# Two-layer decoder trunk on one core: convolution weights taken pair by pair, rotary angles two stages on, the build's load times reckoned from the release of the buffers

## The chip, the cores and the metric

The kernel runs on one core of a Trainium2 chip. The metric is the device time of one execution in microseconds (us), the median of the runs shown. Three runs of the kernel before took 801.74, 802.57 and 802.96 us.

## The reference, cut to what matters

256 tokens of width 1024 go through two layers, beside a memory of 256 tokens. Everything is float32. The stage around the change is the convolution mixer of layer 0: a projection of the normed tokens to three times 1024 columns (b, c and u), a gate, a causal convolution of three taps down the tokens, a second gate, and a projection back. The rotary angles are used only in layer 1.

```
def short_conv_mixer(h, w_in, w_conv, w_out):
    b_gate, c_gate, u = jnp.split(h @ w_in, 3, axis=-1)
    z = c_gate * u
    conv = lax.conv_general_dilated(
        z, w_conv[:, None, :].astype(z.dtype), window_strides=(1,),
        padding=[(CONV_W - 1, 0)], dimension_numbers=("NWC", "WIO", "NWC"),
        feature_group_count=D_MODEL)
    return (b_gate * conv) @ w_out

...
    for l in range(DEPTH):
        h = rms_norm(x, norm_mix[l])
        if l < N_A:
            x = x + short_conv_mixer(h, conv_w_in[l], conv_w[l], conv_w_out[l])
        else:
            j = l - N_A
            x = x + moba_attention(h, moba_w_q[j], moba_w_o[j], cos, sin, k_blk, v_blk, k_mean)
        x = x + mem_cross_attention(rms_norm(x, norm_mem[l]), rms_norm(mem, norm_memkv[l]),
                                    mem_w_q[l], mem_w_kv[l], mem_w_o[l])
        x = x + swiglu(rms_norm(x, norm_ffn[l]), ffn_w_gu[l], ffn_w_down[l])
        if l == N_A - 1:
            k_blk, v_blk, k_mean = shared_kv(x, kv_norm, w_kv, cos, sin)
    return rms_norm(x, norm_final)
```

## The kernel before, in words

Every weight is used once, in chunks of 128 x 1024 float32 values (512 KB), in one order for the whole program: the list `plan` (built above line 415). A chunk passes through four stations.

- **Load.** `load_chunk` (line 347) issues the DMA on SP's queue into one of five buffers (`RAWS`), named `raw_wc`, `raw_wu` and so on. A buffer comes free when the low half of the chunk five places earlier has been made.
- **High half.** ACT casts the chunk to the type fp32r that TensorE multiplies in: `hi_wc` (`split_high`, line 367).
- **Low half.** DVE subtracts the high half from the chunk: `lo_wc` (`split_low`). High and low halves lie in ten pairs of buffers (`WBUFS`).
- **Product.** TensorE makes each product out of three: activation high by weight high, activation low by weight high, activation high by weight low. The activations are split in the same way, ACT casting and DVE subtracting; `mix` holds the normed tokens of the convolution, high and low.

All matmuls are recorded at one line, 315 (`mm`), all transposes at 319, nearly all work of ACT and DVE at 103 (a wrapper), all loads at 332. So groups are told apart by the names of their tiles.

**What sets the order.** Each engine works through its row strictly in order, and the row is fixed when the program is built. The build keeps a clock of its own, by a cost per instruction (`Clock`, line 45): `free["pe"]` is "now", `writes` says when a tile will be ready. After each matmul it calls `Side.poll` (line 138), which steps the side jobs (generators for normalising, gating, copying out of PSUM) whose time has come; a job that yields a number asks to be stepped that many ns later, and `hold` (line 156) makes one wait until a buffer is free by the build's clock. `poll` then calls `Feed.pump` (line 206), which puts the next low half into DVE's row or the next high half into ACT's row if the build's clock has its input ready by then and the engine free. `Feed.take` (line 221) is what the matmuls call: it returns a chunk's two halves and, if they are not in the rows yet, puts them there at once, with all chunks ahead of them.

**The convolution** (`short_conv`, line 875) runs over four pairs of column groups `jp`. A pair has six chunks: two each of `wc`, `wu` and `wb` (512 rows x 256 columns). The loop inside runs over the two columns `jj` of the pair, 128 wide: the matmuls of c into one of two PSUM banks `cu`, those of u into the other, those of b into a bank `pb`. When the c and u sums stand, the jobs `gate_sum` and `conv` copy both banks out (ACT copies the first token half, DVE adds the second product part: `conv <- cu`), which frees them for the next column; then come the gate, the taps and the second gate. The stage starts while the keys of the memory (`memk`) are still being made: the four `pt_h` are transposes of the normed tokens, one set for each quarter of `mix`. `pt_c` transposes two small tables, the gains (`g_rows`) and the taps (`cw_rows`); their job is `tables` (line 783).

**The angles** (`angles`, line 804) load the 256 positions, multiply them by 16 constants that GpSimd writes, reduce the result to the range of the sine with short DVE instructions on `ang` and `turns`, and take sines by ACT, which needs a table load first. The job is started at line 1337, ahead of the convolution, and asks for 15000 ns before it reads the positions. `start_rstd` (line 608) squares the memory for its norm and asks for 9000 ns first.

Behind the convolution come its output projection (`cout`), the values of the memory (`memv`), the memory attention (`mq`, `mo`) and the feed-forward layer (`swiglu`): eleven steps `jp` of two columns each, with gate and up chunks `wg` and `wu`, sums in the same two PSUM banks (now named `gu`), copies `gu_sb`, and the down projection `wd`. Layer 1 has the same stages with the block attention in place of the convolution.

Of the kernel before, what the change touches and what calls it, by code (L numbers as in the profile page):

```python
# [107 lines left out]
class Side:  # L108
# [47 lines left out]
    def hold(self, kind):  # L156

        free = self.free[kind]
        while not free or min(free) > self.clock.now:
            yield 0 if not free else min(free) - self.clock.now  # L160
        free.remove(min(free))
# [11 lines left out]
class Feed:  # L173
# [3 lines left out]
    def __init__(self, clock, items, load, high, low):  # L177
        self.clock, self.items, self.load, self.high, self.low = clock, items, load, high, low
        self.loaded = self.highs = self.lows = self.taken = self.freed = 0
        self.raw, self.ready = {}, {}  # L180
        self.hooks = {}
        self.limit = 5
# [16 lines left out]
    def next_low(self):  # L199
        n = self.lows  # L200
        self.low(self.items[n], self.raw.pop(n), *self.ready[n])
        self.lows += 1
        self.load_to(self.lows + RAWS)
# [51 lines left out]
def yoco_kernel(  # L255
# [23 lines left out]
    clock = Clock()  # L279
# [5 lines left out]
    def acc_tile(name):  # L285
        return ps_acc.tile([P, 512], F32, tag="acc", name=name)
# [44 lines left out]
    def load(dst, src, queue=None):  # L331
        (queue or nc.sync).dma_start(dst, src)
        clock.free["dma"] = max(clock.free["dma"], clock.now + 1100)
        clock.note("dma", 1.43 * math.prod(dst.shape[1:]), [dst], [], 900)
# [12 lines left out]
    def load_chunk(it):  # L347
# [3 lines left out]
        for i in range(it["pieces"]):  # L351
            load(raw[:, :, i * n:(i + 1) * n], src[:, :, i * n:(i + 1) * n])
# [255 lines left out]
    def start_rstd():  # L608
        yield 9000
# [194 lines left out]
    def angles():  # L804
# [6 lines left out]
        yield 15000  # L811
# [62 lines left out]
    def short_conv(act, into):  # L874
# [35 lines left out]
        for jp in range(4):  # L910
            wc, wu, wb = ([feed.take(f"{name}_{jp}_{g}") for g in range(2)] for name in ("wc", "wu", "wb"))
            for jj in range(2):
# [3 lines left out]
                for w in (wc, wu):  # L916
                    side.grab("gu")
                    cus.append(gu_tile("cu"))
                    mm_cols(cus[-1], act, w, jj, 0)
                pb = acc_tile("pb").rearrange("p (r t) -> p r t", r=2)  # L920
                mm_cols(pb, act, wb, jj, 0, (0,))
                for i, w in enumerate((wc, wu)):
                    mm_cols(cus[i], act, w, jj, 1)
# [413 lines left out]
    side.start(angles())  # L1337
    side.finish(x_job[0])
    short_conv(in_mix.act, in_mem0)
    memv0 = mem_values("memv0", mT0)  # L1340
# [28 lines left out]
```

## Time and profile before

| what | value |
|---|---|
| median of three runs | 802.57 us (801.74 to 802.96) |
| the profiled execution | 804.97 us, of which the span is 803.2 us |
| busy share of the span: TensorE (PE) | 98% (789.1 us) |
| weight loads into TensorE (PEld, beside PE) | 86% |
| DVE / ACT / GpSimd (POOL) | 66% / 54% / 2% |
| TensorE's granted clock, mean over the span | 0.993 of full speed |
| read from HBM | 142.64 MB, 182 GB/s with what is written |

The span is the time from the first to the last recorded instruction of the profiled execution; its own time holds 1.8 us around that. A clock of 1.00 is 2.4 GHz; the other level is 1.2 GHz, and a mean between them says for what part of a stretch each was granted. Idle time of an engine in the timeline stands in brackets behind the instruction that ended it, with what that instruction waited for last.

### The profile page before, as it was taken

Reading aid. Unit: us, or ns where it says so; the run is one execution under the profiler, and the core shown is the slowest. Engines: PE = TensorE matmul, PEld = TensorE weight load, DVE = VectorE, ACT = ScalarE, POOL = GpSimd, SP = SyncE. Lnnn points to the kernel's source line nnn. Section 1 sums busy time; section 2 is a strip of 40 time slices with the busy share of each in tenths; the row PEclk is TensorE's granted clock in tenths of the full one; section 3 lists DMA queues with packets and bytes.
Section 4 is the critical chain, followed back from the end, with each engine's and each line's share of the span. In section 5 each row is a group of like instructions: output and inputs, shape, how many; then the busy total and the mean of one; then the engine's idle time right before and its main releaser. Section 6 shows DMA issues by size and latency. Waiting matters only on the chain.

```text
span 803.2 us, 11672 instructions
## 1 busy us (share of the span) xinstructions
PE 789.1 (98%) x4477; PEld 690.6 (86%) x4477; DVE 532.7 (66%) x830; ACT 436.8 (54%) x727; POOL 17.8 (2%) x44
## 2 busy tenths in 40 slices
PE   8899999999999999999999999999999999999996
PEld 8888788898898888888888889888989988888885
DVE  5888788666756656665765667877757555665553
ACT  6656646565645445554655664556645544554442
POOL 0100001000000000000010000010000000000000
PEclk9999999999999999999999999999999999999999
DMA  9666685833536654666474535667344465466611
GB/s 332 196 191 213 215 269 190 280 136 105 173 97 224 213 185 157 188 212 208 153 236 172 170 106 168 226 206 243 119 121 155 156 212 180 158 203 214 209 55 53
DMA packets 91085, 146.55 MB, mean 182 GB/s; under 512 B 4941, under 2 KB 70549, under 8 KB 90773
## 3 DMA queue, kind: packets, MB, share of 16 engines
q1 hardware_dynamic: 90276, 142.92, 54.8%
q0 software_dynamic: 288, 2.10, 0.7%
q8 instruction: 35, 0.57, 0.3%
q10 hardware_dynamic: 464, 0.79, 0.3%
q14 instruction: 22, 0.17, 0.1%
HBM read 142.64 MB, written 3.15 MB: 182 GB/s over the span
## 4 chain that ended last, share of the span: by engine, by line
PE 88%; DMA 5%; DVE 3%; ACT 2%; issue 1%; SPq 0%; POOLq 0%; ACTq 0%; DVEq 0%
PE gu L315 30%; PE ff L315 14%; PE q_acc L315 6%; PE acc_memv L315 5%; PE acc_mo L315 5%; PE acc_memk L315 3%; PE acc_v L315 3%; PE acc_q L315 3%; PE acc_k L315 3%; PE acc_o L315 3%; PE acc_cout L315 3%; PE cu L315 2%; DMA raw_wu<-in_conv_w_in_dram 2%; PE po L315 2%; PE s L315 2%
## 5 line engine op out<-in xcount | busy, mean ns | idle before, releaser
L315 PE MATMUL ff<-hi_wd,guT 128*128 128x512 f32 (+1 forms) x352 | 107.6, 387 | 0.0
L103 DVE TENSOR_TENSOR gu_sb<-gu_sb,gu 128x256 f32<-128x256 f32 x72 | 30.1, 421 | 97.0 <-ACT gu_sb L103 96.2
L103 ACT COPY gu_sb<-gu 128x256 f32<-128x256 f32 x72 | 26.4, 371 | 101.6 <-PE gu L315 101.5
L315 PEld LDWEIGHTS ff<-hi_wd,guT 128*128 128x128 f32 x352 | 65.9, 188 | 12.2
L103 ACT CAST hi_wu<-raw_wu 128x1024 fp32r<-128x1024 f32 x52 | 54.6, 1050 | 33.5 <-DMA raw_wu<-in_ffn_w_gu_dram 23.0
L315 PE MATMUL gu<-ffn,hi_wg 128*128 128x512 f32 x288 | 71.9, 391 | 0.4 <-DVE gu_sb L103 0.4
L315 PE MATMUL gu<-ffn,hi_wu 128*128 128x512 f32 x288 | 71.2, 389 | 0.0
L315 PE MATMUL ff<-lo_wd,guT 128*128 128x512 f32 (+1 forms) x176 | 68.5, 389 | 0.0
L103 DVE TENSOR_TENSOR lo_wu<-raw_wu,hi_wu 128x1024 fp32r<-128x1024 f32 x52 | 62.8, 1219 | 4.6 <-ACT hi_wu L103 4.5
L315 PEld LDWEIGHTS gu<-ffn,hi_wu 128*128 128x128 f32 x288 | 54.1, 188 | 11.3
L315 PEld LDWEIGHTS gu<-ffn,hi_wg 128*128 128x128 f32 x288 | 53.6, 188 | 11.6 <-DVE gu_sb L103 0.8
L103 DVE TENSOR_TENSOR lo_wd<-raw_wd,hi_wd 128x1024 fp32r<-128x1024 f32 x44 | 53.1, 1219 | 0.0
L103 DVE TENSOR_TENSOR lo_wg<-raw_wg,hi_wg 128x1024 fp32r<-128x1024 f32 x44 | 52.2, 1219 | 0.7 <-ACT hi_wg L103 0.5
L103 ACT CAST hi_wd<-raw_wd 128x1024 fp32r<-128x1024 f32 x44 | 45.6, 1050 | 2.8 <-DMA raw_wd<-in_ffn_w_down_dram 2.8
L315 PE MATMUL acc_memk<-mT,hi_memk 128*128 128x256 f32 x256 | 46.7, 287 | 0.0
L103 ACT CAST hi_wg<-raw_wg 128x1024 fp32r<-128x1024 f32 x44 | 44.6, 1051 | 0.6 <-PE acc_mo L315 0.6
L315 PEld LDWEIGHTS gu<-ffn,lo_wg 128*128 128x128 f32 x288 | 39.3, 190 | 2.8
L315 PE MATMUL acc_mo<-hi_mo,oT_mem 128*128 128x512 f32 x128 | 41.2, 397 | 0.2 <-DVE oT_mem L103 0.2
L315 PE MATMUL gu<-ffn,lo_wu 128*128 128x256 f32 x288 | 40.4, 283 | 0.0
L315 PE MATMUL gu<-ffn,lo_wg 128*128 128x256 f32 x288 | 40.2, 282 | 0.0
L315 PE MATMUL acc_memv<-hi_memv,mT 128*128 128x512 f32 x128 | 39.7, 391 | 0.0
L315 PEld LDWEIGHTS acc_memk<-mT,hi_memk 128*128 128x128 f32 x256 | 39.5, 193 | 0.2
(230 smaller groups left out, 1722.3 us busy)
## 6 DMA issues: line engine op xcount, KB each, us to landing
raw_wg<-in_ffn_w_gu_dram SPq DMA_DIRECT2D x44, 512.0 KB, 5.7
raw_wu<-in_ffn_w_gu_dram SPq DMA_DIRECT2D x44, 512.0 KB, 3.6
raw_wd<-in_ffn_w_down_dram SPq DMA_DIRECT2D x44, 512.0 KB, 4.8
raw_memv<-in_mem_w_kv_dram SPq DMA_DIRECT2D x16, 512.0 KB, 4.9
raw_mq<-in_mem_w_q_dram SPq DMA_DIRECT2D x16, 512.0 KB, 5.3
raw_mo<-in_mem_w_o_dram SPq DMA_DIRECT2D x16, 512.0 KB, 5.4
raw_memk<-in_mem_w_kv_dram SPq DMA_DIRECT2D x14, 512.0 KB, 5.4
raw_wc<-in_conv_w_in_dram SPq DMA_DIRECT2D x8, 512.0 KB, 3.8
```

What stands on the lines that cost most here:

```text
L103: return call(out, *args, **kw)
L315: nc.tensor.matmul(o, l, r, start=start, stop=stop)
```

## The change

It has five parts.

- **Weights pair by pair.** `short_conv` took all six chunks of a pair at its top. Now `conv_w` takes two chunks when the first matmul that needs them is written: wc, then wu, then wb.
- **Angles.** `side.start(angles())` moves from ahead of the convolution to behind it, so the job runs beside the first value projection; its first wait drops from 15000 to 4000 ns.
- **Loads in the build's clock.** `Feed` notes in `emptied` when the low half that frees a buffer is done, and `load` starts its reckoning of that chunk's DMA no earlier than that (`freed`). Chunks of column weights (`rows=False`) are reckoned at 1.9 ns a value where it was 1.43.
- **`hold`** no longer waits again if the build's clock has not moved since it last looked.
- **`start_rstd`** asks for 7000 ns where it asked for 9000.

```
--- before.py
+++ after.py
@@ -156,7 +156,9 @@
     def hold(self, kind):
 
         free = self.free[kind]
-        while not free or min(free) > self.clock.now:
+        seen = None
+        while not free or min(free) > self.clock.now != seen:
+            seen = self.clock.now if free else None
             yield 0 if not free else min(free) - self.clock.now
         free.remove(min(free))
 
@@ -178,6 +180,7 @@
         self.clock, self.items, self.load, self.high, self.low = clock, items, load, high, low
         self.loaded = self.highs = self.lows = self.taken = self.freed = 0
         self.raw, self.ready = {}, {}
+        self.emptied = 0.0
         self.hooks = {}
         self.limit = 5
 
@@ -200,6 +203,7 @@
         n = self.lows
         self.low(self.items[n], self.raw.pop(n), *self.ready[n])
         self.lows += 1
+        self.emptied = self.clock.last
         self.load_to(self.lows + RAWS)
 
     def pump(self, soon):
@@ -328,10 +332,10 @@
         side.poll()
         mm(o, a[0], b[0], False, stop, ns)
 
-    def load(dst, src, queue=None):
+    def load(dst, src, queue=None, rows=True, freed=0.0):
         (queue or nc.sync).dma_start(dst, src)
-        clock.free["dma"] = max(clock.free["dma"], clock.now + 1100)
-        clock.note("dma", 1.43 * math.prod(dst.shape[1:]), [dst], [], 900)
+        clock.free["dma"] = max(clock.free["dma"], clock.now + 1100, freed + 1100)
+        clock.note("dma", (1.43 if rows else 1.9) * math.prod(dst.shape[1:]), [dst], [], 900)
 
 
 
@@ -349,7 +353,7 @@
         src = it["src"].rearrange("(a p) n -> p a n", p=P)
         n = it["b"] // it["pieces"]
         for i in range(it["pieces"]):
-            load(raw[:, :, i * n:(i + 1) * n], src[:, :, i * n:(i + 1) * n])
+            load(raw[:, :, i * n:(i + 1) * n], src[:, :, i * n:(i + 1) * n], rows=it["a"] == 1, freed=feed.emptied)
         return raw
 
     def split(hi, lo, src):
@@ -606,7 +610,7 @@
         rstd_from(ss, m_rs[:, h:h + 1])
 
     def start_rstd():
-        yield 9000
+        yield 7000
         yield from mem_rstd(m0, 0)
         yield
         yield from mem_rstd(m1, 1)
@@ -808,7 +812,7 @@
         pos_i = const.tile([P, 2], I32, name="pos_i")
         with nc.allow_non_contiguous_dma(reason="256 positions"):
             nc.sync.dma_start(pos_i, positions[0].rearrange("(h p) -> p h", p=P))
-        yield 15000
+        yield 4000
         pos_f = const.tile([P, 2], F32, name="pos_f")
         vector.tensor_copy(pos_f, pos_i)
         ang = const.tile([P, 2, HR], F32, name="ang")
@@ -908,19 +912,26 @@
             yield
 
         for jp in range(4):
-            wc, wu, wb = ([feed.take(f"{name}_{jp}_{g}") for g in range(2)] for name in ("wc", "wu", "wb"))
+            taken = {}
+
+            def conv_w(name):
+                if name not in taken:
+                    taken[name] = [feed.take(f"{name}_{jp}_{g}") for g in range(2)]
+                return taken[name]
+
             for jj in range(2):
                 j = 2 * jp + jj
                 pieces = [feat.tile([P, T], F32, tag=f"f{i}", name=f"conv{i}") for i in range(2)]
                 jobs, cus = [], []
-                for w in (wc, wu):
+                for name in ("wc", "wu"):
                     side.grab("gu")
                     cus.append(gu_tile("cu"))
-                    mm_cols(cus[-1], act, w, jj, 0)
+                    mm_cols(cus[-1], act, conv_w(name), jj, 0)
                 pb = acc_tile("pb").rearrange("p (r t) -> p r t", r=2)
+                wb = conv_w("wb")
                 mm_cols(pb, act, wb, jj, 0, (0,))
-                for i, w in enumerate((wc, wu)):
-                    mm_cols(cus[i], act, w, jj, 1)
+                for i, name in enumerate(("wc", "wu")):
+                    mm_cols(cus[i], act, conv_w(name), jj, 1)
                     if jj:
                         feed.free(2)
                     jobs.append(side.start(gate_sum(cus[0], pieces[0]) if i == 0 else conv(j, cus[1], pieces, jobs)))
@@ -1334,9 +1345,9 @@
     in_mem0, in_mem1, in_moba = Plain("mem0", "mem0"), Plain("mem1", "mem1"), Plain("moba")
     in_ffn0, in_ffn1 = Normed("ffn0", norm_ffn[0]), Normed("ffn1", norm_ffn[1])
 
-    side.start(angles())
     side.finish(x_job[0])
     short_conv(in_mix.act, in_mem0)
+    side.start(angles())
     memv0 = mem_values("memv0", mT0)
     mem_attention(0, memk0, memv0, in_mem0, in_ffn0)
     swiglu(0, in_ffn0, residual(in_moba))
```

The last three parts change only numbers in the build's clock; what they do is seen in the rows of the engines. Names are those of the program, with the pair, the half of the rows (0 or 1) and a running number. Lines of the changed kernel are four higher than before.

**The start of the convolution.** ACT's row from the first high halves of the first pair's wu on, before:

```order
L103 CAST hi_wu_0_467<-raw_wu_0_406 128x1024
L103 CAST hi_wu_1_486<-raw_wu_1_443 128x1024
L103 CAST mix_0_292<-pt_h 128x4x128
L103 CAST memk_u_482<-k_sb 128x2x256
L103 CAST hi_wb_0_517<-raw_wb_0_462 128x1024
L103 CAST mix_1_293<-pt_h 128x4x128
L103 CAST hi_wb_1_562<-raw_wb_1_501 128x1024
```

and now:

```order
L103 CAST hi_wu_0_484<-raw_wu_0_402 128x1024
L103 CAST memk_u_489<-k_sb 128x2x256
L103 CAST mix_1_297<-pt_h 128x4x128
L103 CAST hi_wu_1_523<-raw_wu_1_453 128x1024
L103 CAST hi_wb_0_556<-raw_wb_0_461 128x1024
L103 CAST memk_u_489<-k_sb 128x2x256
L103 CAST hi_wb_1_588<-raw_wb_1_506 128x1024
```

The last cast of `mix` (the second row of that name) stood behind the first `hi_wb`; now both `hi_wb` and the second `hi_wu` stand behind it. On TensorE the same place, before:

```order
L315 MATMUL acc_memk_3_184<-mT_1_114,lo_memk_7_420 128x256
L315 MATMUL cu<-mix_0_292,hi_wc_0_431 128x512 x4
L315 MATMUL cu<-mix_1_293,hi_wc_1_445 128x512 x4
L315 MATMUL cu<-mix_0_292,hi_wu_0_467 128x512
L319 MATMUL pt_c<-ident,g_rows_541 128x32
L319 MATMUL pt_c<-ident,cw_rows 128x24
L315 MATMUL cu<-mix_0_292,hi_wu_0_467 128x512 x3
L315 MATMUL cu<-mix_1_293,hi_wu_1_486 128x512 x4
L315 MATMUL pb<-mix_0_292,hi_wb_0_517 128x512
```

and now:

```order
L319 MATMUL acc_memk_3_184<-mT_1_114,lo_memk_7_420 128x256
L319 MATMUL cu<-mix_0_296,hi_wc_0_437 128x512 x4
L319 MATMUL cu<-mix_1_297,hi_wc_1_467 128x512 x4
L319 MATMUL cu<-mix_0_296,hi_wu_0_484 128x512 x4
L319 MATMUL cu<-mix_1_297,hi_wu_1_523 128x512 x2
L323 MATMUL pt_c<-ident,g_rows_543 128x32
L323 MATMUL pt_c<-ident,cw_rows 128x24
L319 MATMUL cu<-mix_1_297,hi_wu_1_523 128x512 x2
L319 MATMUL pb<-mix_0_296,hi_wb_0_556 128x512
```

The transposes `pt_c` stood behind one matmul of the second weight, wu; now they stand behind six of it. Ahead of the rows shown, the fourth set of transposes `pt_h` had 12 matmuls of `memk` between itself and the first `cu`; now it has 28. On SP the loads keep their order but for that of the positions, which stood between the two loads of the second pair's wc and now stands behind the third load of `mq`.

**The second and third pair.** DVE's row around the third pair's first column (pairs count from 0 in the names, so `lo_wu_2` is the third pair's), before:

```order
L103 TENSOR_TENSOR lo_wc_2_1_815<-raw_wc_2_1_774,hi_wc_2_1_814 128x1024
L103 TENSOR_TENSOR conv0_870<-conv0_870,cu_872 128x256
L103 TENSOR_TENSOR conv1_871<-conv1_871,cu_886 128x256
L103 TENSOR_TENSOR conv0_870<-conv0_870,conv1_871 128x256
L103 TENSOR_TENSOR lo_wu_2_0_833<-raw_wu_2_0_777,hi_wu_2_0_832 128x1024
L103 TENSOR_TENSOR lo_wu_2_1_854<-raw_wu_2_1_780,hi_wu_2_1_853 128x1024
L103 TENSOR_TENSOR lo_wb_2_0_945<-raw_wb_2_0_783,hi_wb_2_0_944 128x1024
L103 TENSOR_TENSOR lo_wb_2_1_964<-raw_wb_2_1_864,hi_wb_2_1_963 128x1024
```

and now:

```order
L103 TENSOR_TENSOR lo_wc_2_1_805<-raw_wc_2_1_746,hi_wc_2_1_804 128x1024
L103 TENSOR_TENSOR yT_0_562<-conv1_752,yT_0_562 128x256
L103 TENSOR_TENSOR lo_wu_2_0_831<-raw_wu_2_0_767,hi_wu_2_0_830 128x1024
L103 TENSOR_TENSOR conv0_838<-conv0_838,cu_840 128x256
L103 TENSOR_TENSOR lo_wu_2_1_853<-raw_wu_2_1_782,hi_wu_2_1_852 128x1024
L103 TENSOR_TENSOR conv1_839<-conv1_839,cu_857 128x256
L103 TENSOR_TENSOR conv0_838<-conv0_838,conv1_839 128x256
L103 TENSOR_TENSOR lo_wb_2_0_893<-raw_wb_2_0_786,hi_wb_2_0_892 128x1024
```

Here `conv <- cu` is the second half of a copy out of a `cu` bank. `lo_wu_2_1`, whose end lets the load of the fourth pair's `raw_wu_3_0` go out, stood behind both copies and their product; now it stands between the two. On ACT `hi_wu_3_0` stands ahead of both copies of the next column, as before, and the sines and the table load, which stood in ACT's row of this pair, have gone to the value projection.

**A feed-forward step.** ACT's row in the fifth step of layer 0, before:

```order
L103 CAST hi_wu0_4_0_2793<-raw_wu0_4_0_2702 128x1024
L103 CAST hi_wu0_4_1_2803<-raw_wu0_4_1_2760 128x1024
L103 COPY gu_sb0_2764<-gu_2766 128x256
L103 COPY gu_sb1_2765<-gu_2785 128x256
L103 ACTIVATE gu_sb0_2764<-gu_sb0_2764 128x256
L103 CAST guT0_1_2609<-gu_sb1_2765 128x256
```

and now:

```order
L103 CAST hi_wu0_4_0_2793<-raw_wu0_4_0_2697 128x1024
L103 COPY gu_sb0_2764<-gu_2766 128x256
L103 CAST hi_wu0_4_1_2822<-raw_wu0_4_1_2760 128x1024
L103 COPY gu_sb1_2765<-gu_2785 128x256
L103 ACTIVATE gu_sb0_2764<-gu_sb0_2764 128x256
L103 CAST guT0_1_2609<-gu_sb1_2765 128x256
```

The high half of the second chunk of wu stood ahead of both copies out of the banks; now it stands between them. This is so in 14 of the 22 steps of the two layers.

## Rows read from the trace of the kernel before

**Rows 1.** TensorE's waits: what waits <- for whom: us in all, times, longest.
```profile
PE cu L315 <- DVE mix L103: 2.2, 1, 2.2
PE cu L315 <- DVE conv L103: 2.1, 1, 2.1
```

**Rows 2.** Stretches: from:to, length, busy PE, PEld, DVE, ACT, POOL; granted clock, DMA share, GB/s.
```profile
34.65:37.04 2.39, 0.19 (x2) 0.00 (x1) 0.75 (x2) 2.31 (x3) 0.00 (x0) 1.00 0.72 226
37.04:42.09 5.05, 5.05 (x15) 3.81 (x16) 5.05 (x6) 1.75 (x3) 0.00 (x0) 0.66 0.44 124
79.92:82.21 2.29, 0.18 (x2) 0.01 (x1) 0.48 (x2) 1.83 (x4) 0.00 (x0) 1.00 1.06 353
82.21:87.57 5.36, 5.36 (x16) 4.28 (x17) 4.94 (x10) 2.10 (x5) 0.00 (x0) 0.68 0.10 31
```

**Rows 3.** Timeline, ACT and DVE ahead of the first wait: start, us, instruction.
```profile
34.73 1.04 ACT L103 CAST hi_wb<-raw_wb 128x1024 fp32r<-128x1024 f32 x1 [2.50 <-DMA raw_wb<-in_conv_w_in_dram]
35.68 0.58 ACT L103 CAST mix<-pt_h 128x512 fp32r<-128x512 f32 x1
...
36.29 0.69 DVE L103 TENSOR_TENSOR mix<-pt_h,mix 128x512 fp32r<-128x512 f32 x1 [2.13 <-ACT mix L103]
```

**Rows 4.** Timeline, ACT and DVE ahead of the second wait.
```profile
64.44 1.06 ACT L103 CAST hi_wu<-raw_wu 128x1024 fp32r<-128x1024 f32 x1 [0.68 <-DMA raw_wu<-in_conv_w_in_dram]
...
68.50 1.28 ACT L103 ACT_TABLE_LOAD   x1
...
71.80 2.35 DVE L103 TENSOR_TENSOR lo_wu<-raw_wu,hi_wu 128x1024 fp32r<-128x1024 f32 x2
...
80.38 1.04 ACT L103 CAST hi_wu<-raw_wu 128x1024 fp32r<-128x1024 f32 x1 [2.82 <-DMA raw_wu<-in_conv_w_in_dram]
```

**Rows 5.** Timeline, SP's queue: loads issued.
```profile
31.29 1.54 SPq L332 DMA_DIRECT2D g_rows<-in_norm_mem_dram  x1
...
34.23 0.40 SPq L332 DMA_DIRECT2D raw_wc<-in_conv_w_in_dram  x1
...
74.22 1.47 SPq L332 DMA_DIRECT2D raw_wu<-in_conv_w_in_dram  x2
```

**Rows 6.** Timeline, TensorE around the first wait.
```profile
31.88 0.60 PE L319 MATMUL pt_h<-ident,hn 128*128 128x128 f32 x4
...
33.74 1.09 PE L315 MATMUL cu<-mix,hi_wc 128*128 128x512 f32 x4
...
38.41 0.31 PE L319 MATMUL pt_c<-ident,g_rows 32*128 32x32 f32 x1
```

**Rows 7.** Timeline, TensorE in the third pair's first column.
```profile
67.11 1.12 PE L315 MATMUL cu<-mix,lo_wc 128*128 128x256 f32 x8
```

**Rows 8.** DMA issues from 31.2 to 35.5 us: count, KB each, us to landing.
```profile
raw_wc<-in_conv_w_in_dram SPq DMA_DIRECT2D x1, 512.0 KB, 3.8
g_rows<-in_norm_mem_dram SPq DMA_DIRECT2D x1, 8.0 KB, 5.1
```

**Rows 9.** Timeline, DVE, TensorE and ACT: an angle's instruction, the first value projection.
```profile
59.65 0.19 DVE L103 SCALAR_TENSOR_TENSOR ang<-turns,ang 128x32 f32<-128x32 f32 x1
...
126.31 3.67 DVE L103 SCALAR_TENSOR_TENSOR lo_memv<-raw_memv,g_cols,hi_memv 128x1024 fp32r<-128x1024 f32 x3
...
132.09 0.39 PE L315 MATMUL acc_memv<-lo_memv,mT 128*128 128x512 f32 x1
...
135.60 1.28 DVE L103 SCALAR_TENSOR_TENSOR lo_memv<-raw_memv,g_cols,hi_memv 128x1024 fp32r<-128x1024 f32 x1
...
137.39 1.28 DVE L103 SCALAR_TENSOR_TENSOR lo_memv<-raw_memv,g_cols,hi_memv 128x1024 fp32r<-128x1024 f32 x1
...
143.06 1.31 ACT L103 ACTIVATE memv<-acc_memv,m_rs 128x512 fp32r<-128x512 f32 x2 [5.99 <-PE acc_memv L315]
```

**Rows 10.** Timeline, ACT and TensorE in a feed-forward step of layer 1.
```profile
754.85 1.06 ACT L103 CAST hi_wu<-raw_wu 128x1024 fp32r<-128x1024 f32 x1 [1.31 <-DMA raw_wu<-in_ffn_w_gu_dram]
...
761.08 1.98 PE L315 MATMUL gu<-ffn,hi_wu 128*128 128x512 f32 x8
```

More of the change, by code (lines that the diff above doesn't have):

```diff
@@ L158, in hold @@
         free = self.free[kind]
-        while not free or min(free) > self.clock.now:
+        seen = None
+        while not free or min(free) > self.clock.now != seen:
+            seen = self.clock.now if free else None
             yield 0 if not free else min(free) - self.clock.now
@@ L180, in __init__ @@
         self.raw, self.ready = {}, {}
+        self.emptied = 0.0
         self.hooks = {}
@@ L202, in next_low @@
         self.lows += 1
+        self.emptied = self.clock.last
         self.load_to(self.lows + RAWS)
@@ L329, in mm3, with load @@
         mm(o, a[0], b[0], False, stop, ns)
-    def load(dst, src, queue=None):
+    def load(dst, src, queue=None, rows=True, freed=0.0):
         (queue or nc.sync).dma_start(dst, src)
-        clock.free["dma"] = max(clock.free["dma"], clock.now + 1100)
-        clock.note("dma", 1.43 * math.prod(dst.shape[1:]), [dst], [], 900)
+        clock.free["dma"] = max(clock.free["dma"], clock.now + 1100, freed + 1100)
+        clock.note("dma", (1.43 if rows else 1.9) * math.prod(dst.shape[1:]), [dst], [], 900)
     def row_plan(name, w, c0, gain=None, pieces=1, halves=1):
@@ L351, in load_chunk @@
         for i in range(it["pieces"]):
-            load(raw[:, :, i * n:(i + 1) * n], src[:, :, i * n:(i + 1) * n])
+            load(raw[:, :, i * n:(i + 1) * n], src[:, :, i * n:(i + 1) * n], rows=it["a"] == 1, freed=feed.emptied)
         return raw
@@ L910, in short_conv, with conv_w @@
         for jp in range(4):
-            wc, wu, wb = ([feed.take(f"{name}_{jp}_{g}") for g in range(2)] for name in ("wc", "wu", "wb"))
+            taken = {}
+            def conv_w(name):
+                if name not in taken:
+                    taken[name] = [feed.take(f"{name}_{jp}_{g}") for g in range(2)]
+                return taken[name]
             for jj in range(2):
@@ L915, in short_conv @@
                 jobs, cus = [], []
-                for w in (wc, wu):
+                for name in ("wc", "wu"):
                     side.grab("gu")
                     cus.append(gu_tile("cu"))
-                    mm_cols(cus[-1], act, w, jj, 0)
+                    mm_cols(cus[-1], act, conv_w(name), jj, 0)
                 pb = acc_tile("pb").rearrange("p (r t) -> p r t", r=2)
+                wb = conv_w("wb")
                 mm_cols(pb, act, wb, jj, 0, (0,))
-                for i, w in enumerate((wc, wu)):
-                    mm_cols(cus[i], act, w, jj, 1)
+                for i, name in enumerate(("wc", "wu")):
+                    mm_cols(cus[i], act, conv_w(name), jj, 1)
                     if jj:
```

6 lines of the change are left out of this document (3 added, 3 removed).

## The prediction, made before the changed kernel ran

> **What bounds the kernel now.** I read the page's busy shares first, then TensorE's waits, then stretches around the two longest, then the timelines of the engines behind them. TensorE is busy 98% of the span, as the table above has it: only what it waits for, or does at a lowered clock, can be won. Two waits stand out, both in the short convolution, of 2.2 and 2.1 us [rows 1]; the reader is to see that both name DVE, which only passes on a delay. The stretches [rows 2] give their whole price. From 34.65 to 37.04 TensorE issues nothing new: 2.39 us. The next 5.05 us run at a mean granted clock of 0.66, so 5.05 x 0.34 = 1.72 us more are lost. From 79.92 to 82.21 it is 2.29 us, and 5.36 x 0.32 = 1.72 us in the stretch behind. Together 8.12 us, 1% of the run, is all that this change can reach. A difference of 0.2%, 1.6 us, is about what a measurement of this kernel can tell from none.
>
> What is late each time? The first wait is for the last quarter of the normed activations: TensorE needs its low half, which DVE makes at 36.29 out of a high half that ACT makes at 35.68, because ACT stood until 34.73 before a high half of wb whose load had not landed [rows 3]. ACT works its row strictly in order, so a weight that TensorE needs much later held back an activation it needed at once: the build had put all six chunks of the pair into the row when the first was wanted. In the second, ACT stands until 80.38 before a high half of wu [rows 4], and behind it stand the two copies that empty the PSUM banks TensorE wants. That load was issued at 74.22 [rows 5] and took 6.16 us; it could not go out earlier because its buffer was released by the low halves of wu, which DVE did only at 71.80. And they were late because ACT was busy with a table load at 68.50 for the rotary angles [rows 4] while DVE's next row waited for it.
>
> **The change, part by part.** *Weights pair by pair, first wait.* In the new order TensorE's last transposes of the normed rows stand 28 matmuls ahead of the convolution instead of 12. Before, they began at 31.88 and the convolution at 33.74 [rows 6], so 12 matmuls and 4 transposes took 1.86 us; 16 matmuls more at no more than 0.13 put them at about 29.9, done at 30.4. ACT's last cast no longer has hi_wb ahead of it: 0.58 us [rows 3], done near 31.0. DVE's low half then has one low half of wc ahead of it (2.35 for two of that size [rows 4], so 1.2) and one of memk, which is as large as mix's (0.69, and its own 0.69 behind it), so it ends by about 33.6. TensorE needs it behind four matmuls, at 34.65 (the four from 33.74 on take 0.228 each). Margin 1 us: the wait of 2.39 goes, and with it, as I take it, the lowered clock behind: 4.11 us.
>
> *Second wait.* Everything from there on runs 4.1 us earlier on TensorE, so the loads must be earlier too. The low half of wu that frees the buffer now stands right behind the first column sum of its column, ahead of the second. That sum needs the matmuls that ended at 67.11 + 1.12 = 68.2 [rows 7], now 64.1; a copy and a sum of 128x256, 0.8 us (the wait for the second ended so: ACT's high half out at 81.4, TensorE on at 82.21): 64.9. Its high half ended at 65.5 [rows 4] and can hardly be later than that now. So the low half runs from 65.5 at worst, 1.2 us, and the load goes out at 66.7 instead of 74.22. With the old 6.16 us it lands at 72.9, the high half ends at 73.9, copies and sums at 74.9. TensorE wants the bank at 79.92 - 4.11 = 75.8. Margin 0.9 us at worst. The order of ACT itself has not changed there: hi_wu still stands ahead of both copies, so this rests on the load alone. I take the 2.29 and the 1.72 as gone: 4.01 us. What is late next is this same load, by a margin of 0.9.
>
> *A new wait.* The two small transposes for the gain and tap columns (pt_c) move from behind one matmul of the second weight to behind six: TensorE reaches them at 33.74 + 14 x 0.228 = 36.9, where the old stall had let it come at 38.41 [rows 6]. Their loads go out behind a load of wb that waits for the low half of the first wc; DVE now has one more activation low half ahead of that one (0.69 us, some 0.6 in a row [rows 3]). The first of the small loads was issued at 31.29, the big one behind all of them at 34.23 [rows 5]; they landed 5.1 and 3.8 us later [rows 8], at 36.4 and 38.0, and the last small one lies between. Moved by 0.6 that is 37.0 to 38.6, against 36.9: a wait of 0.1 to 1.7 us, at the upper end with a lowered clock behind (1.7 + 1.72 = 3.4). The last small load has 12 KB (24 x 128 values) and follows the first directly, so it is nearest to the low end: I take 0.2 us.
>
> *Rotary angles two stages on.* From the convolution go twelve short DVE instructions (0.19 us [rows 9]) and the table load with four activations; they come back in the first value projection. Most stand ahead of the last low half there, which ended at 137.39 + 1.28 = 138.7. Twelve times 0.19 make that 141.0 at worst; TensorE begins this projection at 132.09 and takes six matmuls a chunk, so it wants the eighth at 132.09 + 42 x 0.228 = 141.7 [rows 9]. ACT has 5.99 us of idle time behind its squares there, ahead of 143.06, for a table load of 1.28. On SP the positions' load now stands behind the third load of query weights, which goes out once the low halves begun at 126.31 are through, at 130.0. Even if it takes 5.1 us, as the small load above, it lands at 135.1, and DVE converts the positions behind the second last low half (135.60 + 1.28 [rows 9]), at about 136.8. GpSimd's 16 constants move along between two of its powers, and nothing but the angles reads them. So I cost all this at nothing; the cover is 0.7 us on DVE and 1.7 us on the load, and past these TensorE would wait for the excess.
>
> *Loads timed from their buffers' release.* It only changes the build's own clock, and so what it puts where: in each feed-forward step ACT's high half of the second wu chunk now stands between the two copies, and DVE's low half ahead of the activation's. TensorE's row there has no idle time ahead of it (761.08 [rows 10]): cost nothing, see the last rival. No load changes its place on SP but the positions', and no instruction is added or dropped on TensorE.
>
> Sum: 2.39 + 1.72 + 2.29 + 1.72 - 0.2 = 7.9 us. The profiled execution took 804.97 us (span 803.2), so a profiled one of the changed kernel would take 797.1. The runs' median is 802.57, 2.40 below the profiled execution; taking the same off it gives 794.7.
>
> **Rivals.** *The second wait stays* (0.08): the load lands after more than 7.1 us instead of 6.16, and hi_wu still stands ahead of the copies. For it speaks that TensorE now asks for the same weights 4 us sooner; against it, that the load goes out 7.5 us sooner. Saved: 2.39 + 1.72 - 0.2 = 3.9, 798.7.
>
> *The small transposes hold TensorE* (0.08), at the upper bound: 8.12 - 3.4 = 4.7 saved, 797.9.
>
> *The clock does not hang on the waits* (0.04). The stretches show it at 1.00 up to the end of either wait and lowered right behind [rows 2], which is why I count 3.44 us for it; if it fell for another reason, only the waits go: 4.68 - 0.2 = 4.5, 798.1. The Trainium skill, "TensorE: Matmul & The Clock Gate", section "HAM oscillation — how this bites in real kernels", ties a fall to gaps of the array longer than these two; by that rule neither wait of 2.3 us would have lowered the clock, and the 3.44 us would stay. This trace does not agree with it: the lowered clock begins right behind each of these gaps.
>
> *Runs without a profile hold less of it* (0.08): if the 2.40 us between the profiled execution and the median all lie in these waits, 7.9 - 2.4 = 5.5 are saved, 797.1.
>
> *Slower* (0.03): in the feed-forward layers. The high half of wu that ACT waits for (1.31 us, until 754.85 [rows 10]) now stands between the copy of the gate bank and that of the up bank, at 14 places of the two layers. Should its load land later than now, the up copy is late with it. TensorE takes that bank again at 761.08; copy and sum ahead of it need 0.8 us and the high half 1.06, so nothing shows until the load lands at 759.2, 4.4 us later than it did. Past that point every microsecond counts 14 times: 1 us gives 802.57 - 7.9 + 14 = 808.7. Against it: DVE's low half stands earlier in its row, so the next load goes out earlier.
>
> **How the numbers follow.** The forecast has 0.69 and gives 794.7; its own range, from no new wait with the spread of the runs shown to a wait of 1.7 without a lowered clock, is 793.2 to 796.4. Adding the two rivals at 797.1 and 797.9 and the clock's at 798.1 leaves out 0.11; the range is 793.2 to 798.2. All these and the 798.7 are faster by over 0.2%: with the forecast 0.97, of which I leave 0.02 to a wait that none of them names and that eats most of the gain. So faster 0.95, within 0.2% 0.02, slower 0.03.
>
> **What would show it.** Right: among TensorE's waits the lines on mix and conv are gone; the stretches of the convolution stand at a clock of 1.00; the two copies behind the fourth pair's first high half of wu come near 74 and ACT waits less than 1 us ahead of that high half; the table load stands past 120 us, with no wait of TensorE near it; and all behind the convolution stands about 8 us earlier. Wrong: a line on pt_c of over 0.5 us, a wait on conv that stays, a clock below 1.00 somewhere between 30 and 100 us without a wait ahead of it, or a new line on gu in both feed-forward layers.

## The result and the profile after

The changed kernel took 796.93 us (median of four runs, 796.64 to 797.55), the kernel before 802.15 us (four runs, 800.34 to 802.96); the ratio is 0.9939, 95% interval 0.9920 to 0.9958. That is 5.2 us less where 7.9 were forecast; the time lies inside the forecast range and 2.2 us above the forecast itself. The two profiled executions stand further apart: 804.97 before, 796.64 now, 8.3 us.

TensorE's waits in the changed kernel (what waited <- for whom, us in all, times, longest):

```profile
PE warm L323 <- POOL neg_half L525: 1.4, 1, 1.4
PE pt_m L323 <- DMA m<-in_mem_dram: 0.5, 1, 0.5
PE acc_mo L319 <- DVE oT_mem L103: 0.2, 1, 0.2
PE pt_r L323 <- ACT qT L103: 0.2, 1, 0.2
```

Both lines of [rows 1] are gone, and none on `pt_c` or `gu` has come. Stretches of the changed kernel (columns as in [rows 2]):

```profile
34.64:38.05 3.41, 3.41 (x16) 2.56 (x15) 3.14 (x6) 1.90 (x3) 0.00 (x0) 1.00 0.72 204
75.90:79.75 3.85, 3.85 (x18) 3.19 (x17) 3.78 (x8) 0.78 (x2) 0.00 (x0) 1.00 0.53 184
```

Where [rows 2] had 0.66 and 0.68, the granted clock is 1.00. The run cut in two where the first value projection begins, before, and then the second part of the changed kernel:

```profile
0.00:132.09 132.09, 125.73 (x735) 111.21 (x736) 100.75 (x169) 80.27 (x131) 6.09 (x31) 0.97 0.72 233
132.09:803.20 671.11, 663.35 (x3743) 579.42 (x3741) 431.97 (x662) 356.48 (x596) 11.76 (x13) 1.00 0.53 173
```

```profile
124.05:794.90 670.85, 663.43 (x3743) 579.36 (x3741) 431.79 (x674) 357.07 (x601) 11.75 (x13) 1.00 0.53 172
```

In the changed kernel the projection begins at 124.05 (132.09 in [rows 9]), and 794.9 - 124.05 = 670.85 us are left. So 8.04 of the 8.3 us lie ahead of it, where the two waits and their lowered clock stood; all that stands behind it, the feed-forward layers with their changed ACT and DVE rows among it, took 0.3 us less and lost nothing.

The timeline of the changed kernel, TensorE, then ACT, DVE and SP (start, us, instruction):

```profile
33.73 2.00 PE L319 MATMUL cu<-mix,hi_wc 128*128 128x512 f32 x8
...
37.03 0.24 PE L323 MATMUL pt_c<-ident,g_rows 32*128 32x32 f32 x1
...
75.90 1.98 PE L319 MATMUL cu<-mix,hi_wc 128*128 128x512 f32 x8
...
124.05 0.39 PE L319 MATMUL acc_memv<-lo_memv,mT 128*128 128x512 f32 x1
...
30.71 0.58 ACT L103 CAST mix<-pt_h 128x512 fp32r<-128x512 f32 x1
...
71.07 1.06 ACT L103 CAST hi_wu<-raw_wu 128x1024 fp32r<-128x1024 f32 x1 [0.74 <-DMA raw_wu<-in_conv_w_in_dram]
72.62 0.37 ACT L103 COPY conv<-cu 128x256 f32<-128x256 f32 x1 [0.49 <-PE cu L319]
73.58 0.37 ACT L103 COPY conv<-cu 128x256 f32<-128x256 f32 x1 [0.59 <-PE cu L319]
...
128.74 1.28 ACT L103 ACT_TABLE_LOAD   x1
...
31.80 0.68 DVE L103 TENSOR_TENSOR mix<-pt_h,mix 128x512 fp32r<-128x512 f32 x1
...
131.14 1.28 DVE L103 SCALAR_TENSOR_TENSOR lo_memv<-raw_memv,g_cols,hi_memv 128x1024 fp32r<-128x1024 f32 x1
...
66.31 2.29 SPq L336 DMA_DIRECT2D raw_wu<-in_conv_w_in_dram  x2
```

The last cast of `mix` is done at 31.3 and its low half at 32.5; TensorE asks at 34.64. The load of the fourth pair's wu goes out at 66.31 where it went out at 74.22 [rows 5], and its high half begins at 71.07 where it began at 80.38 [rows 4]. The copies now wait for TensorE, not TensorE for them.

### The profile page after: what moved, and what is told of

Its sections match the earlier page's. It is cut to its first block, busy times and chain, and to the rows that moved or that the text cites. A ratio compares the mean times of both kernels' runs of the same rounds, so it can differ in the third digit from the quotient of the medians.

```text
span 794.9 us, 11651 instructions
## 1 busy us (share of the span) xinstructions
PE 785.6 (99%) x4477; PEld 688.7 (87%) x4477; DVE 531.0 (67%) x830; ACT 435.9 (55%) x727; POOL 18.0 (2%) x44
## 4 chain that ended last, share of the span: by engine, by line
PE 98%; DMA 0%; DVE 0%; ACT 0%; POOLq 0%; issue 0%; ACTq 0%
PE gu L319 31%; PE ff L319 15%; PE acc_memk L319 6%; PE q_acc L319 6%; PE cu L319 6%; PE acc_memv L319 5%; PE acc_mo L319 5%; PE pb L319 3%; PE acc_v L319 3%; PE acc_k L319 3%; PE acc_o L319 3%; PE acc_cout L319 3%; PE acc_q L319 3%; PE po L319 2%; PE s L319 2%; PE pt_h L323 1%
```

## The experiments

Two theories stood against each other. A is the prediction's: taking the weights pair by pair frees the cast of `mix`, and the angles' move helps the second wait. B holds that the loads' reckoning, costed at nothing in the prediction, moves the rows. Medians are given beside that of before in the same job, which differs from job to job (801.80, 802.35, 803.45 and 801.96 us).

### The same kernels once more

> The kernel before, unchanged, once more. The profiled execution of before took 804.97 us, while its four other runs took 800.34 to 802.96 and those of the changed kernel only 796.64 to 797.55. Theory (the two waits of the convolution, and the lowered clock behind them, differ from execution to execution, because both end with the landing of a load): the times spread over 2 us or more again, the granted clock of the runs lies between 0.992 and 0.997, longer where it is lower, and the new profile shows waits of TensorE on mix and conv that differ by over 0.5 us from 2.2 and 2.1. Rival (the waits are fixed, and only that one execution was disturbed elsewhere): waits of 2.2 and 2.1 again, within 0.2, and times within 1 us of each other.

Twelve runs: 802.12 us (801.39 to 805.12), ratio 1.0011 (0.9999 to 1.0023). The profiled execution took 801.39. Its waits and stretches:

```profile
PE cu L315 <- DVE mix L103: 1.9, 1, 1.9
...
PE cu L315 <- DVE conv L103: 0.6, 1, 0.6
```

```profile
34.73:36.80 2.07, 0.17 (x2) 0.00 (x1) 0.75 (x2) 2.07 (x3) 0.00 (x0) 1.00 0.69 194
36.80:41.84 5.04, 5.04 (x15) 3.81 (x16) 5.04 (x6) 1.89 (x3) 0.00 (x0) 0.66 0.53 153
79.84:80.48 0.64, 0.01 (x1) 0.00 (x0) 0.47 (x2) 0.64 (x3) 0.00 (x0) 1.00 0.97 309
80.48:86.00 5.52, 5.51 (x30) 4.83 (x31) 5.10 (x10) 2.44 (x7) 0.00 (x0) 1.00 0.36 110
```

The same program had 2.39 and 2.29 us of standing TensorE in [rows 2] and 2.07 and 0.64 here, and the short one lowered no clock. That is 2.39 - 2.07 + 2.29 - 0.64 = 1.97 of waits and one lowered stretch of 1.7, 3.7 us in all; the spans differ by 803.2 - 799.6 = 3.6. So the waits do differ between executions, and both end with a load: the one on conv by 1.5 us, the one on `mix` by 0.3, less than the 0.5 expected. The granted clock of the runs lay between 0.993 and 0.998 and does not order their times, though the theory had them longer where it is lower: one of 803.44 us had 0.998. That mean takes in the end of the run, where a lowered clock delays nothing: in this execution it is 0.50 from 797.0 to 799.6 us, behind TensorE's last matmul (792.8).

> The changed kernel, unchanged, once more, beside the runs of before on the same chip. Theory (its gain is the two waits, and none of what is left ends with a load): no wait of TensorE in the convolution, clock 0.997 or more in every run, times within 1.5 us of each other around 797, and 4 to 6 us less than before. Rival (the loads-only kernel's 797.77 is the same time, and the two cannot be told apart): its median between 797.3 and 798.2.

797.34 us (796.50 to 797.53) beside 802.35, ratio 0.9951 (0.9935 to 0.9966); no wait in the convolution. The six times spread over 1.0 us where the 24 of before in this job spread over 5.7 (798.83 to 804.49). The rival's 797.3 to 798.2 holds as well: by these times the changed kernel cannot be told from the one with the loads' reckoning alone, told below (797.77, ratio 0.9949).

### One part alone

The edits are the hunks of the change, each put into the kernel before by itself. For the pairwise taking:

```
-            wc, wu, wb = ([feed.take(f"{name}_{jp}_{g}") for g in range(2)] for name in ("wc", "wu", "wb"))
+            taken = {}
...
+                    mm_cols(cus[-1], act, conv_w(name), jj, 0)
```

> Before, with the pairwise taking of the convolution's weights alone. Theory A (the prediction's: this part takes the first wait away): no wait on mix, and about 4 us less than before (2.4 of wait, 1.7 of clock). Theory B (the loads' reckoning is what moves the row, this part does nothing there): ACT's row still has the last cast of mix behind hi_wb, so a wait on mix of 1.5 to 2.4 us stays and the time is within 1 us of before.

Slower: 805.87 us (804.69 to 807.10) beside 801.80, ratio 1.0054 (1.0039 to 1.0069). Its waits:

```profile
PE cu L315 <- DVE mix L103: 1.9, 1, 1.9
PE cu L315 <- DVE lo_wu L103: 1.6, 1, 1.6
...
PE pb L315 <- DVE lo_wb L103: 0.8, 2, 0.4
```

ACT's row ahead of the first of them, and a stretch around the last two:

```profile
35.27 1.05 ACT L103 CAST hi_wb<-raw_wb 128x1024 fp32r<-128x1024 f32 x1 [2.11 <-DMA raw_wb<-in_conv_w_in_dram]
36.23 0.58 ACT L103 CAST mix<-pt_h 128x512 fp32r<-128x512 f32 x1
```

```profile
60.00:72.00 12.00, 9.61 (x43) 7.76 (x42) 9.63 (x22) 6.35 (x14) 0.00 (x0) 0.86 0.55 175
```

Theory A falls: hi_wb still stands ahead of the last cast of `mix`, and the wait is still there. B's "within 1 us of before" falls too, for new waits have come in the second pair's first column, 12 - 9.61 = 2.4 us, with 12 x 0.14 = 1.7 us of lowered clock. ACT and DVE there:

```profile
58.22 1.05 ACT L103 CAST hi_wc<-raw_wc 128x1024 fp32r<-128x1024 f32 x1 [2.23 <-DMA raw_wc<-in_conv_w_in_dram]
59.17 0.51 ACT L103 ACTIVATE conv<-conv,cw 128x256 f32<-128x256 f32 x1
...
59.71 1.00 DVE L103 SCALAR_TENSOR_TENSOR conv<-conv,cw,conv 128x255 f32<-128x255 f32 x2 [2.95 <-ACT conv L103]
...
61.20 1.22 DVE L103 TENSOR_TENSOR lo_wu<-raw_wu,hi_wu 128x1024 fp32r<-128x1024 f32 x1
```

A high half of the third pair's wc now stands ahead of a tap of the first pair on ACT. While its load is out, the tap waits, DVE waits 2.95 us for the tap, and behind it wait the low halves that TensorE needs now.

For the angles:

```
-        yield 15000
+        yield 4000
...
-    side.start(angles())
     side.finish(x_job[0])
     short_conv(in_mix.act, in_mem0)
+    side.start(angles())
```

> Before, with the rotary angles moved behind the convolution alone. Theory A: the table load is out of the way of the low halves of wu, so the second wait (2.1 us) goes and the first stays: about 4 us less than before where before has its full waits, 2 to 3 by the medians. Theory B agrees on the first wait but holds that the second is set by the order of ACT around hi_wu: both high halves of the fourth pair's wu still stand ahead of the copies here, so a wait on conv of 0.5 to 2 us stays, and at most 2 us are gained.

798.76 us (797.27 to 801.47), ratio 0.9973 (0.9959 to 0.9986): faster by 3.0 us by the medians, as A had it for the second wait. The profiled execution (797.27, the fastest) has no wait on conv at all, against B's 0.5 to 2 us, and this on `mix`, where both theories had the full wait stay:

```profile
PE cu L315 <- DVE mix L103: 0.3, 1, 0.3
```

ACT's row at that place is that of before. What differs is the landing: the two loads of wb, issued from 28.0 on in all three profiled executions, took 6.0 us (median of the two) in the first profile of before, 5.7 in its second and 4.7 here, in this order:

```profile
raw_wb<-in_conv_w_in_dram SPq DMA_DIRECT2D x2, 512.0 KB, 6.0
```

```profile
raw_wb<-in_conv_w_in_dram SPq DMA_DIRECT2D x2, 512.0 KB, 5.7
```

```profile
raw_wb<-in_conv_w_in_dram SPq DMA_DIRECT2D x2, 512.0 KB, 4.7
```

The twelve times fall into two groups, 797.3 to 798.8 and 800.6 to 801.5, as they would if this wait is now short and now long.

For the loads' reckoning:

```
-        clock.free["dma"] = max(clock.free["dma"], clock.now + 1100)
-        clock.note("dma", 1.43 * math.prod(dst.shape[1:]), [dst], [], 900)
+        clock.free["dma"] = max(clock.free["dma"], clock.now + 1100, freed + 1100)
+        clock.note("dma", (1.43 if rows else 1.9) * math.prod(dst.shape[1:]), [dst], [], 900)
```

> Before, with the loads reckoned from the release of their buffers (and column chunks at 1.9 ns a value) alone: weights still taken six at once, angles where they were, 9000 ns kept. Theory A: it moves nothing that counts, the first wait stays, within 1 us of before. Theory B: in this order the last cast of mix stands ahead of the first hi_wb and the copies of the third pair ahead of hi_wu, so both waits are gone: no wait of TensorE over 0.5 us in the convolution, clock 0.997 or more, and the time of the changed kernel, 796 to 798 us.

797.77 us (796.64 to 798.03), ratio 0.9949 (0.9935 to 0.9963), and no wait of TensorE in the convolution: B, in full. This part alone gives 4.0 us by the medians. ACT's row at the places of the two waits:

```profile
32.72 0.59 ACT L103 CAST mix<-pt_h 128x512 fp32r<-128x512 f32 x1 [1.01 <-PE pt_h L321]
33.20 1.05 ACT L103 CAST hi_wb<-raw_wb 128x1024 fp32r<-128x1024 f32 x1
...
72.83 0.37 ACT L103 COPY conv<-cu 128x256 f32<-128x256 f32 x1 [2.59 <-PE cu L317]
...
74.05 0.38 ACT L103 COPY conv<-cu 128x256 f32<-128x256 f32 x1
...
74.62 1.06 ACT L103 CAST hi_wu<-raw_wu 128x1024 fp32r<-128x1024 f32 x1
```

The last cast of `mix` stands ahead of hi_wb, and both copies out of the `cu` banks stand ahead of the fourth pair's first hi_wu. `pump` puts a high half into the row when the build's clock has its load landed; with the landing reckoned later, the cast and the copies come first. Which of this part's two changes does it, the release or the 1.9 ns, was not tried.

For the earlier norm:

```
-        yield 9000
+        yield 7000
         yield from mem_rstd(m0, 0)
```

> Before, with 7000 for 9000 ns in start_rstd alone. The squares of the memory come earlier in ACT's row, and with them the transposes of the normed rows: the last cast of mix stands ahead of hi_wb, but behind both high halves of wu; the fourth pair's row is as in before. Theory (each part that pulls the cast ahead of hi_wb shortens the first wait, none is needed alone): a wait on mix under 1 us, the one on conv as in before (0.6 to 2.1), 798 to 801 us. Rival (only the reckoning of the loads or the angles move it): a wait on mix of 1.9 to 2.4 stays, 801 to 803 us.

800.81 us (799.65 to 802.86) beside 803.45, ratio 0.9970 (0.9954 to 0.9985). The wait on `mix` is gone, and three short ones on conv are left:

```profile
PE cu L315 <- DVE conv L103: 2.0, 3, 0.8
```

### One part left out, or two kept

From the changed kernel, the loads' reckoning taken back:

```
-        clock.free["dma"] = max(clock.free["dma"], clock.now + 1100, freed + 1100)
-        clock.note("dma", (1.43 if rows else 1.9) * math.prod(dst.shape[1:]), [dst], [], 900)
+        clock.free["dma"] = max(clock.free["dma"], clock.now + 1100)
+        clock.note("dma", 1.43 * math.prod(dst.shape[1:]), [dst], [], 900)
```

> The changed kernel with the loads reckoned as before (1.43 ns a value, not from the release), all else of the change kept. Theory B (the loads' reckoning carries the gain): in ACT's row both high halves of the first pair's wu stand ahead of the last cast of mix again, and both of the fourth pair's wu ahead of the copies; a wait on mix of 0.5 to 2 us comes back and one on conv of 0.3 to 1.5 us, and the time is 799 to 803 us. Theory A (taking pair by pair and the moved angles carry it): no wait over 0.3 us, within 0.7 us of the changed kernel.

797.78 us (797.42 to 798.82), ratio 0.9955 (0.9938 to 0.9972): B's 799 to 803 was wrong, and no wait on `mix` came back. A's "no wait over 0.3" was wrong too, for there are short waits:

```profile
PE cu L317 <- DVE conv L103: 0.7, 1, 0.7
PE pt_c L321 <- DMA g_rows<-in_norm_mix_dram: 0.5, 1, 0.5
PE acc_memk L317 <- DVE lo_memk L103: 0.5, 1, 0.5
```

Among them is the wait on `pt_c` that the prediction feared. None lowers the clock, and beside the changed kernel's 797.34 of the same job this is 0.4 us. So the loads' reckoning is enough by itself, but not needed where the other four parts are made. That the angles' move and the earlier norm do it among these follows only from what each did alone; `hold` was in no run by itself.

From the changed kernel, the pairwise taking taken back:

```
-                    taken[name] = [feed.take(f"{name}_{jp}_{g}") for g in range(2)]
...
+            wc, wu, wb = ([feed.take(f"{name}_{jp}_{g}") for g in range(2)] for name in ("wc", "wu", "wb"))
```

> The changed kernel with the convolution's weights taken six at once again, all else of the change kept. Theory B' (taking pair by pair adds nothing once the loads are reckoned from the release and the angles are gone: the last cast of mix stands ahead of hi_wb in this row too): no wait over 0.3 us in the convolution and within 0.6 us of the changed kernel, 796.5 to 797.9. Theory A (this part took the first wait away): a wait on mix of over 1 us comes back, 799 us or more.

797.39 us (796.53 to 797.80), ratio 0.9928 (0.9905 to 0.9950), no wait in the convolution. The pairwise taking adds nothing that these runs can tell.

From the changed kernel, the angles put back (15000 ns again):

```
+    side.start(angles())
     side.finish(x_job[0])
     short_conv(in_mix.act, in_mem0)
-    side.start(angles())
```

> The changed kernel with the angles ahead of the convolution again (15000 ns), all else kept. Theory (with the loads reckoned right, the first wait is gone either way; the twelve short instructions and the table load still push low halves in the second and third pair late, as in the pairwise-only kernel): waits on the low halves of wu or wb of 0.5 to 1.5 us in all, no lowered clock, 797.5 to 799.5 us. Rival (the angles' place is what took the second wait away): a wait on conv or on a low half of over 1.9 us with a lowered clock behind it, 800 us or more.

799.22 us (798.40 to 799.46), ratio 0.9954 (0.9935 to 0.9973), 1.8 us above the kernel of the run just told:

```profile
PE pb L319 <- DVE lo_wb L103: 1.0, 2, 0.6
```

The clock stays at 1.00 there, as the theory had it. Low halves are late in the second pair's first column again, as with the pairwise taking alone. That the pairwise taking is the cause here too is not shown: the loads' part alone has no such wait with the angles at the same place, but it lacks the earlier norm and `hold` as well.

Into the kernel before, the two hunks of the loads and of the angles, as shown above:

```
+        clock.free["dma"] = max(clock.free["dma"], clock.now + 1100, freed + 1100)
...
     short_conv(in_mix.act, in_mem0)
+    side.start(angles())
```

> Before, with the loads' reckoning and the moved angles alone (weights six at once, 9000 ns, hold as before). Theory (these two parts are enough: the reckoning puts the last cast of mix ahead of hi_wb and the angles leave the second and third pair): no wait over 0.5 us in the convolution, clock 1.00 there, and the time of the changed kernel, 796.5 to 797.9 us. Rival (the earlier norm is needed too, since here the last cast of mix comes later in the row): a wait on mix of 0.5 to 1.5 us, 798 to 800 us.

796.97 us (796.61 to 797.30) beside 801.96, ratio 0.9941 (0.9926 to 0.9955), no wait in the convolution. The two parts give what all five give.

### The lowered clock

The changed kernel, with a wait put in:

```
+            for _ in range(late):
+                nc.scalar.copy(junk, x_sb[:, 0, :512])
```

> The changed kernel with nine copies of 128x512 added in ACT's row right ahead of the last cast of mix; their result is not used. At 0.48 us each they hold the cast back by 4.3 us. In the changed kernel the low half ended at 32.5 and TensorE wanted it at 34.6, so a wait on mix of about 2.2 us comes back at 34.6. Theory (the lowered clock follows from the wait): 5 us behind it at a granted clock of 0.6 to 0.7, and 2.2 + 1.7 = 3.9 us more than the changed kernel. Rival (the clock fell for another reason, such as the load on TensorE in that stage): the clock stays at 1.00 and it is 2.2 us more.

802.04 us (801.58 to 802.62), against 797.34 for the changed kernel in the same job: 4.7 more.

```profile
34.97:37.94 2.97, 0.00 (x1) 0.00 (x0) 0.74 (x2) 2.91 (x5) 0.00 (x0) 1.00 0.00 0
37.94:42.99 5.05, 5.05 (x16) 3.60 (x17) 5.05 (x8) 3.09 (x5) 0.00 (x0) 0.66 0.47 131
```

The wait is longer than expected, 2.97 us, for the nine copies took 5.82 us and not 4.3; with 5.05 us at 0.66 behind it (1.72 lost) that makes 4.69. And the kernel before, with its first wait filled:

```
+                    for i in range(8):
+                        x_both = act.units[0][:, i % 4].rearrange("p r t -> p (r t)")
+                        nc.tensor.matmul(cus[1].rearrange("p r t -> p (r t)"), wc[0][0][:, i % 4, :P], x_both,
+                                         start=True, stop=True)
```

> Before, with eight matmuls of 128x512 added on TensorE at the place of the first wait, into the bank that the next products overwrite; nothing reads them. They take 8 x 0.227 = 1.8 us of a wait of 1.9 to 2.4. Theory (the lowered clock follows from TensorE standing still): the wait on mix shrinks to under 0.6 us, the products behind it still start where they did, and the clock stays at 1.00 up to 43 us, so 1.7 us less in the convolution's first column than in before. Rival: the clock falls to 0.7 there all the same, and nothing is gained.

```profile
34.57 1.98 PE L923 MATMUL cu<-mix,hi_wc 128*128 128x512 f32 x8
36.39 1.17 PE L315 MATMUL cu<-mix,hi_wc 128*128 128x512 f32 x4
...
39.90 1.11 PE L315 MATMUL cu<-mix,lo_wc 128*128 128x256 f32 x8
```

```profile
36.39:39.90 3.51, 3.51 (x17) 2.64 (x16) 3.51 (x4) 1.85 (x3) 0.00 (x0) 1.00 0.37 110
```

The products that took 5.05 us behind the wait in [rows 2], and 5.04 in the second profile of before, take 3.51 when TensorE had work in the wait. By the medians it is 800.69 beside 802.35, but the ratio, 0.9997 (0.9980 to 1.0015), leaves the sign open: the second wait (2.0 us in its profile) is untouched and varies more than this gains. So the profile decides, not the time. A shorter first wait in this execution does not explain it, for the low half of `mix` was late here too:

```profile
35.62 0.69 DVE L103 TENSOR_TENSOR mix<-pt_h,mix 128x512 fp32r<-128x512 f32 x1 [1.59 <-ACT mix L103]
```

It ended at 36.31, so without the eight matmuls TensorE would have stood still for some 1.7 us from 34.57 on; the pairwise-only kernel stood for 1.60 us up to 62.47, and its clock was lowered behind. And behind the second wait of this same execution, which nothing fills, the clock falls:

```profile
79.95:85.00 5.05, 5.05 (x15) 4.06 (x16) 4.52 (x10) 2.21 (x5) 0.00 (x0) 0.67 0.18 58
```

The lowered clock follows from TensorE standing still.

## Why the prediction was right, and where it was not

- **What bounds the kernel: right.** All that could be won was the two waits and the clock behind them; 8.04 of 8.12 us went, in the profiled pair.
- **The terms: right in size.** 2.39 and 2.29 of wait are gone. The same products take 3.41 us (from 34.64 to 38.05) where they took 5.05, so the first lowered stretch cost 1.64, not 1.72; behind the second wait it is 3.85 (75.90 to 79.75) against 5.59 (82.21 to 87.80), 1.74. Together 8.06, against 8.04 measured.
- **The part that carries the first wait: wrong.** The prediction put it to the step "Weights pair by pair, first wait" and costed "Loads timed from their buffers' release" at nothing. What moved ACT's cast ahead of hi_wb is the build's reckoning: that step alone takes both waits away, the pairwise taking alone leaves the first and costs 4 us. The reading that failed is "the build had put all six chunks of the pair into the row when the first was wanted". Taken two at a time, hi_wb still stands ahead of the cast (35.27 and 36.23 in the pairwise-only kernel); taken six at once, it stands behind it where the loads are reckoned later. `pump` had put it there ahead of time: in the row before, the cast of `mix` stands between the two hi_wb, while `take` puts in what is missing with nothing between. The order of the whole change showed the cast moved, and that was read as the work of the largest hunk. The earlier norm, not costed at all, takes the first wait away too.
- **The second wait: right in its chain.** The low half, the load (66.31, forecast 66.7), the high half (71.07, forecast 72.9: the load took 4.8 us, not 6.16) and the copies (72.6 and 73.6, forecast near 74) came in that order, and TensorE took the bank at 75.90 (forecast 75.8). The column of [rows 7] is the second pair's second, not the third pair's first (the columns begin at 33.74, 46.58, 54.92, 63.26 and 71.60), but its time was the right one. In their profiled executions the angles alone and the loads alone both have no wait on conv, in two ways: the first by an earlier load, with hi_wu still ahead of the copies; the second by the copies standing ahead of hi_wu, with the table load still in the convolution (62.62).
- **pt_c, the angles, the feed-forward rows: right.** TensorE came to `pt_c` at 37.03 (forecast 36.9) and did not wait, for which 0.2 had been taken. The table load stands at 128.74 with no wait near it. The last low half of memv is done at 131.14 + 1.28 = 132.4; the forecast's 141.0 at worst is 133.0 with all work 8 us earlier. The slower rival's wait on `gu` did not come.
- **From the profiled execution to the median: the step that failed.** "Taking the same off" assumed that 2.40 us lie between profiled execution and median in either kernel. For the kernel before, the traces put them into the waits: its second profiled execution is 3.6 us shorter than the first by shorter waits and one lowered stretch less, so the first had drawn long ones. (That runs without a trace have shorter waits as well is inferred.) The changed kernel has no such waits, and its profiled execution lies 0.3 below its median. So the saving by medians is 5.2, not 7.9. The rival "Runs without a profile hold less of it" named this, with 797.1 against 796.93 measured, and deserved more than 0.08. The measured median lies in the range only because that rival was taken into it: the forecast's own ended at 796.4. Its name is the wrong reason, though: profiled executions differ among themselves in the same way (804.97 and 801.39).
- **The clock rival: wrong, and settled.** The two kernels above that put a wait in and fill one both side with the forecast. The Trainium skill, "TensorE: Matmul & The Clock Gate", section "HAM oscillation — how this bites in real kernels", ties the fall to longer gaps; here the clock stood at 0.66 behind gaps of 2.07, 2.39 and 2.97 us, at 0.75 behind one of 1.60 (62.47 to 67.50 in the pairwise-only kernel), and at 1.00 behind 0.64, 0.7 and 0.8, so the measurement decides against it.

What stays open: why the same loads land after 4.7 us in one execution and 6.0 in another. Nothing was tried on that. What the release and the 1.9 ns do apart, and what `hold` does, is open too.

## What to carry to other kernels

When a change has several hunks, build each alone and look where its rows move before crediting one: the hunk that looks like the remedy may do harm by itself, and a number in the planner's clock may do the work. A wait that ends with a load's landing differed here from execution to execution (0.64 and 2.29 us for the second), so take its price from several profiles, not one; with the waits gone the times spread less as well (1.0 us over six runs, 5.7 over 24 before). And a high half that is wanted late must not stand ahead of an activation that is wanted now in an engine that works in order.

## What the runs showed of the hardware that was not expected

Two loads of 512 KB, issued from the same moment on (28.0 us) behind the same loads, took 6.0, 5.7 and 4.7 us to land (median of the two) in three executions. And the price of a wait jumps: 0.64 us of standing TensorE cost 0.64 us (clock 1.00 behind it), 2.29 us of it cost 2.29 + 1.74 (0.68 behind it).
